# A four-branch token mixer: gate and branch products with tokens on the partitions

## The chip, the cores and the metric

The kernel runs on one core of a Trainium2 chip. The metric is the device time of one execution in microseconds. The core has TensorE (matrix products into PSUM), VectorE, ScalarE and GpSimd (elementwise work), and SyncE, which here issues all DMA.

## The reference, cut to what matters

One decoder layer, 256 tokens of 1024 channels. Four mixers A to D turn projections of x into rows of 256 channels; each is projected to 1024 channels, multiplied by a sigmoid gate, which is itself a projection of x, and the four are summed. An output projection, a residual and a layer norm follow, then 32 experts with two chosen per token, and a second layer norm.

```python
p = _split_in(x @ w_in[l])
...
ys = jnp.stack([ya, yb, yc, yd], axis=2)
gates = jax.nn.sigmoid(p["gate"].reshape(bsz, seq, N_BRANCHES, D_MODEL))
merged = jnp.sum(gates * jnp.einsum('bsnc,ncd->bsnd', ys, w_branch[l]), axis=2)
x = _layer_norm(DN_ALPHA * x + merged @ w_out[l], ln_g[l, 0], ln_b[l, 0])
y = _moe(x, ...)
x = _layer_norm(DN_ALPHA * x + y, ln_g[l, 1], ln_b[l, 1])
```

The shapes: `w_in` is 1024 x 7096, of which the last 4096 columns make the gates; `w_branch` 4 x 256 x 1024, `w_out` 1024 x 1024; the experts' three weight arrays are 32 x 1024 x 256 (two) and 32 x 256 x 1024, 96 MiB in all.

## The kernel before, in words

All data are float32. Every projection up to the router is made of three products: each operand is split in two parts (`split`, L356: ScalarE casts to the first part, L366, VectorE subtracts to the second, L367), and `mm3` (L381 to L383) issues low x high, high x low and high x high into the same PSUM bank.

The input projection's weights come as 56 tiles of 128 partitions x 1024 (`TILES`, L191), two per load. The last 32 are the gates, eight per branch in the order B, A, C, D; such a tile holds all 1024 input channels for 128 output channels. With the weights stationary and the 256 tokens of x moving, a tile takes 8 x 3 matmuls of 256 columns. Two tiles share one of the two PSUM banks of the pool `pj`; then ScalarE takes Tanh of half the value into the branch's gate tile `g` (L489), 128 channels per partition row and tokens along the row.

The branch products (`gen_M`, L1160) have the same form: stationary 128 columns of the branch's weight (split by `gen_N`, L1144), moving the branch's two-part output `parts` (256 tokens), four pieces per branch of 12 matmuls, each in a bank of the six-bank pool `px`. A piece is merged on VectorE (L1182: (gate + 1) x product) and added to the sum `mg` (L1185, GpSimd for A and C, VectorE for D). For D each piece of the sum is then split into `mgh` (L1192, ScalarE) and `mgl` (L1194, VectorE). Since channels are on the partitions, these are used as they are as stationary operands of the output projection (`gen_O`, L1313: for every one of eight channel groups 2 x 2 x 3 matmuls of 512 columns, moving the split output weights of `gen_U`).

The router (`gen_R`, one for each half of the tokens) transposes its input on TensorE (L1367), computes logits (L1384), picks experts, counts ranks (L1415) and builds selection matrices; `gen_E` gathers the rows of the first four experts (L1464). The expert loop (from L1553) takes the experts in eight groups of four. Their 1 MiB weights are loaded by `fetch` (L1247), 25 ahead: the first seven into memory that the mixers' pool gives back (step X, L1226), the next sixteen into the ring of 17 slots of 8 KB per partition (`w2`), two into smaller ones. The same 17 slots serve the weight tiles, their split parts, the gates, `parts`, `mg`, `mgh`, `mgl`, the output weights and x.

The order of all work up to the expert loop is written out: `ORDER` (L211) is a string of letters, each of which advances one generator to its next `yield` (P products of the input projection, S its splits and loads, N and M branch weights and products, D, B, A, C the mixers, L the first expert loads, U and O the output projection, Q and R the router). Every engine and SyncE's queue run their instructions in that order, each waiting for its own data and slots.

Of the kernel before, what the change touches and what calls it, by code (L numbers as in the profile page):

```python
# [113 lines left out]
def _layout(inp):  # L114
# [14 lines left out]
    for n in TILES:  # L129
# [5 lines left out]
        if n == "sm":  # L135
            c = sm
        elif n == "ck":
            c = ck
        else:
            o0 = 3000 + 1024 * "ABCD".index(n[1]) + 128 * int(n[2]) if n[0] == "g" else at[n[:-1]] + 128 * int(n[-1])  # L140
            c = W[:, o0:o0 + 128]
# [70 lines left out]
    "PSBYNDSSFSUSSXSSDPRSSQZPCDOSPEPDDDBSDDDDSPDPPDSDPDDSDPDSPPPFSDFPSPDWAFDDPPDPBSDDPDSDDBBDDDPFDDDDDPDP"  # L212
    "SDSWDPDPDBBPPWDSDSBPBBDPDSDBDPCSCDCPBPDDDWDBBMCDDBDDDBWSDSPPBWDDBBSBPDBBDPDDBWDDDDDSDDBDBDBDDBDPBDDP"
    "DBBPDDDSPDDDBDDSPDPBDDDDBDSPDDDDDBDDDDDPNNBNBDDPDDDDDDDDBPAADAANAAAADSDDDDDAASADPPAABDDABABADPBBSAAB"
    "BADADAADDDBBDBAAAAADDBDSDDBDDBBDBBPASBBBBSBBBBDPDBDPBBBCDCPBCCBBBAPSMCMCDCCCCMNCCCPCMCCMSCCCCPPSPPMN"
    "MSPNSMNPSMPSMMPMNCCSPMPSCPDDSPPPCMSSNPMCMSMMLCXPSMLLLLMPLNLNPSMMPSPLPSMMPSMMMPPSNPSPMPSPNSMMLMPPSMMM"
    "PMNPMMLNMPSMSMPMMPMSUUUUUPUMMMMMPPOUULOLLUOSULPMMLMLUUMOLOUUOUUUUOQLOQQQQQQQQQOLLQQQLQQQYYUQQRLQORRQ"
    "RLRRRRQRRRQRRZRQZQERRRRRRRRRLLLREEQQERRE"
# [3 lines left out]
def body(ctx, tc, I, out):  # L222
# [93 lines left out]
    load_tiles(2)  # L316
    SY.dma_start(cst[:, 0:CC["m2"][0]], I["cst"][:, 0:CC["m2"][0]])
    SY.dma_start(csts, I["cst"][:, NMIX:NCC])
# [110 lines left out]
    def gen_S():  # L429
# [16 lines left out]
        for i, n in enumerate(TILES):  # L446
            if i > 1:
                sh = [P, 4, 256] if n[:2] in ("av", "cv") else [P, KT, P]
# [11 lines left out]
    def gen_P():  # L460
        pair = None
        for i, n in enumerate(TILES):
# [3 lines left out]
            if n in ("av1", "cv1"):  # L466
# [8 lines left out]
                continue  # L475
            c = int(n[-1]) % 2 if n[-1].isdigit() else 0
# [5 lines left out]
            if n[0] == "g":  # L482
                m = int(n[2])
                if c:
                    yield 0
                    if m == 1:
                        gslot[n[1]] = slot("g" + n[1], [P, 4, 2, S])
                    gts[n[1], m // 2] = t = gslot[n[1]][:, m // 2]
                    A.activation(t, pair, AF.Tanh, scale=0.5)  # L489
                    if i == len(TILES) - 1:  # L490
                        ready(AF.Sqrt, t[:, 1, 0:1])
            else:
                if i == 0:
                    V.tensor_scalar(omm, pc[:, PC["mu"][0]:PC["mu"][0] + 7], -1.0, 1.0, op0=OP.mult, op1=OP.add)
                if n == "ak0":
                    G.memset(into("ak", [P, 2, 2, S]), 0.0)
# [1284 lines left out]
```

## Time and profile before

| | |
|---|---|
| Time, median of 3 runs | 511.18 us (510.54 to 512.19) |
| The profiled execution's own time | 511.06 us |
| Its span, first to last instruction | 509.3 us |
| TensorE busy | 465.8 us (91%), 4396 matmuls |
| VectorE, ScalarE, GpSimd busy | 239.1, 195.2, 46.5 us |
| DMA moved | 146.79 MB, mean 288 GB/s |
| TensorE's granted clock, mean | 0.973 of 2.4 GHz |

A record of a matmul is longer than the distance to the next one, since matmuls are pipelined: rates are read from starts, not from lengths. The DMA share is the mean busy share of the core's 16 DMA engines. SyncE's rows show when a load is issued, not when it lands. Idle time in brackets stands behind the engine that ended it.

### The profile page before, as it was taken

To read this page: it belongs to the slowest core of one execution; us is meant where nothing else is said; L and a number is where in the kernel's file an instruction comes from. 1 tells how busy PE (TensorE), PEld (TensorE's weight loads), DVE (VectorE), ACT (ScalarE), POOL (GpSimd) and SP (SyncE) were. 2 spreads that over 40 slices of the span, in tenths; PEclk is the share of its full clock that TensorE was granted. 3 is DMA by queue.
4 is the path that set the end of the run, shared out by engine and by line. 5 is a ranking of instruction groups with operands and counts; after the bars stand their busy time and mean duration, and the time that the engine had idled before them with its cause. 6 is when DMAs were issued, how large, how long until landed. Compare 5 with 4: busy or idle time off the path is not lost. (4 is left out here: it accounts for less than half of the span.)

```text
span 509.3 us, 10326 instructions
## 1 busy us (share of the span) xinstructions
PE 465.8 (91%) x4396; PEld 359.1 (71%) x4396; DVE 239.1 (47%) x479; ACT 195.2 (38%) x357; POOL 46.5 (9%) x55
## 2 busy tenths in 40 slices
PE   7999999999999999999999898998988989877891
PEld 6988888998788999999998676553635446324530
DVE  4577657976877468725665543112211122002015
ACT  5778474355586457424444242001202011101311
POOL 2101111500000011411150000000000000000002
PEclk9999999999999999999999979999999999979897
DMA  8979240340242444699679999999999999999952
GB/s 281 390 309 365 93 161 1 97 155 1 81 169 84 166 166 160 241 423 420 257 291 429 382 399 383 420 349 418 419 417 420 420 423 415 421 420 417 389 190 86
DMA packets 27416, 146.79 MB, mean 288 GB/s; under 512 B 3108, under 2 KB 5736, under 8 KB 12264
## 3 DMA queue, kind: packets, MB, share of 16 engines
q1 hardware_dynamic: 27368, 146.11, 72.8%
q8 instruction: 35, 0.57, 0.4%
q14 instruction: 13, 0.11, 0.1%
HBM read 143.48 MB, written 2.62 MB: 287 GB/s over the span
## 5 line engine op out<-in xcount | busy, mean ns | idle before, releaser
L381 PE MATMUL ps<-xl,hl 128*128 128x256 f32 x416 | 122.9, 295 | 2.3 <-ACT hl L366 1.6
L382 PE MATMUL ps<-xh,hl 128*128 128x256 f32 x416 | 119.0, 286 | 1.3 <-DVE hl L367 1.2
L383 PE MATMUL ps<-xh,hl 128*128 128x256 f32 x416 | 118.6, 285 | 0.0
L367 DVE TENSOR_TENSOR hl<-w,hl 128x1024 fp32r<-128x1024 f32 (+1 forms) x75 | 88.0, 1189 | 51.3 <-ACT hl L366 51.0
L381 PEld LDWEIGHTS ps<-xl,hl 128*128 128x128 f32 x416 | 80.7, 194 | 6.9 <-ACT hl L366 2.2
L382 PEld LDWEIGHTS ps<-xh,hl 128*128 128x128 f32 x416 | 80.7, 194 | 3.3 <-DVE hl L367 2.2
L383 PEld LDWEIGHTS ps<-xh,hl 128*128 128x128 f32 x416 | 80.7, 194 | 0.0
L366 ACT CAST hl<-w 128x1024 fp32r<-128x1024 f32 (+1 forms) x75 | 74.0, 1012 | 14.8 <-DMA w<-win 7.5
L1562 PE MATMUL ps<-w,xg 128*32 128x256 f32 x1024 | 66.6, 402 | 7.5 <-DMA w<-mwu 7.5
L1562 PEld LDWEIGHTS ps<-w,xg 128*32 128x32 f32 x1024 | 33.6, 115 | 38.1 <-DMA w<-mwu 10.1
L1464 PE MATMUL ps<-Sel,nrm 128*128 128x128 f32 x256 | 33.8, 288 | 0.9 <-DVE Sel L1457 0.9
L1464 PEld LDWEIGHTS ps<-Sel,nrm 128*128 128x128 f32 x256 | 31.4, 200 | 4.0 <-issue 3.7
L1549 PE MATMUL ps<-small,SGT 128*128 128x512 f32 x48 | 23.7, 616 | 9.3 <-DVE small L1543 5.1
L1543 DVE COPY small<-ps 128x512 f32<-128x512 f32 x6 | 4.1, 692 | 51.4 <-PE ps L1549 51.4
L1514 ACT COPY SGT<-ps 128x256 f32<-128x256 f32 x8 | 3.0, 372 | 63.3 <-PE ps L1512 63.3
L1531 PE MATMUL ps<-w,small 128*32 128x512 f32 x192 | 23.1, 598 | 3.5 <-ACT xg L1471 3.0
L1549 PEld LDWEIGHTS ps<-small,SGT 128*128 128x128 f32 x48 | 8.2, 189 | 25.0 <-DVE small L1543 10.1
L1704 POOL TENSOR_TENSOR res<-res,ln 128x512 f32<-128x512 f32 x1 | 1.6, 1646 | 235.7 <-ACT res L1703 235.7
L1457 DVE TENSOR_TENSOR Sel<-rank,csts 128x128 f32<-128x128 f32 x16 | 4.0, 289 | 31.2 <-PE ps L1512 31.1
L381 PE MATMUL ps<-parts,hl 128*128 128x256 f32 x64 | 18.6, 291 | 0.0
L382 PE MATMUL ps<-parts,hl 128*128 128x256 f32 x64 | 18.1, 283 | 0.0
L383 PE MATMUL ps<-parts,hl 128*128 128x256 f32 x64 | 18.1, 283 | 0.0
(414 smaller groups left out, 685.2 us busy)
## 6 DMA issues: line engine op xcount, KB each, us to landing
w<-mwu SPq DMA_DIRECT2D x32, 1024.0 KB, 15.0
w<-win SPq DMA_DIRECT2D x27, 1024.0 KB, 6.3
w<-mwg SPq DMA_DIRECT2D x27, 1024.0 KB, 13.6
w<-mwd SPq DMA_DIRECT2D x23, 1024.0 KB, 15.0
w<-mwd SPq DMA_DIRECT2D x10, 512.0 KB, 13.3
w<-mwg SPq DMA_DIRECT2D x10, 512.0 KB, 16.4
w<-wbr SPq DMA_DIRECT2D x4, 1024.0 KB, 5.0
w<-wout SPq DMA_DIRECT2D x4, 1024.0 KB, 6.4
```

Of the source, the lines that this page charges most:

```text
L366: A.copy(hi, src)
L367: V.tensor_tensor(lo, src, hi.bitcast(F32), op=OP.subtract)
L381: T.matmul(dst, lhsT=ls[0], rhs=rs[1], start=start, stop=False)
L382: T.matmul(dst, lhsT=ls[1], rhs=rs[0], start=False, stop=False)
L383: T.matmul(dst, lhsT=ls[0], rhs=rs[0], start=False, stop=stop)
L1457: V.tensor_tensor(t, rank[q][:, 4 * g:4 * g + 4, None].broadcast_to([P, 4, 32]), C("iota")[:, None, :].broadcast_to([P, 4, 32]), op=OP.is_ ...
L1464: T.matmul(pg[:, k4], lhsT=nrm[q][:, 128 * k:128 * k + 128], rhs=f2(SelR[g, q]), start=q == 0 and k4 == 0, stop=True, skip_group_check=True)
L1514: A.copy(SGT, pg)
L1531: T.matmul(pd[h][32 * e4:32 * e4 + 32], lhsT=outs[g][0][:, k, 32 * e4:32 * e4 + 32], rhs=wds[g][e4](k)[:, 512 * h:512 * h + 512], start=k ...
L1543: V.tensor_copy(dn[h], pd[h])
L1549: T.matmul(yacc[q, h], lhsT=outs[g][1][:, q], rhs=dn[h], start=False, stop=False, skip_group_check=True)
L1562: T.matmul(pgu[32 * e4:32 * e4 + 32, i], lhsT=xg[:, k, 32 * e4:32 * e4 + 32], rhs=ws[e4](k), start=k == 0, stop=k == KT - 1, tile_position ...
```

## The change

The packed gate weights are laid out anew: a tile now holds 256 input channels for 512 output channels, so that four tiles make one half of a branch's gates. In `gen_P` x is the stationary operand (128 channels x 128 tokens) and the weights move, 512 columns. Tile 0 and tile 1 of a four are multiplied for both halves of the tokens (6 matmuls each), tile 2 waits, and with tile 3 the two last tiles are multiplied for the first half of the tokens (12 matmuls), then for the second half. The two halves of the tokens take both banks of `pj`; Tanh is taken of each when its 12 are through.

In `gen_M` a piece is 512 channels for 128 tokens: 6 matmuls of 512 columns with `parts` as stationary operand. The sum now has tokens on the partitions, so for D each piece is transposed by four TensorE transposes into a PSUM bank, and `mgh` and `mgl` are made from that bank.

At the start one load of two weight tiles becomes two, with a load of constants between them.

`ORDER` is a new string, 644 letters instead of 640. On TensorE its stretches around the last gates are, before: gates D0 and D1, branch product C3 between them, then D0 (branch), gates D2 and D3, D1, gates D4 and D5, D2, D3, gates D6 and D7, projection step 0, and so on without a break to step 5. After: gates D0, product of C's last piece, gates D1, D's first piece, gates D2 and D3 (first and second token half), transposes of the first piece, D's second piece, gates D4, transposes of the second piece, gates D5 to D7, D's third piece, its transposes, D's fourth piece, projection step 0, transposes of the fourth piece, steps 1 to 5. On ScalarE and VectorE the split of output weight 0 stands ahead of the third piece's merge. The step X with the first expert loads stands before gate tile C0 in the old string and behind the four tiles C0 to C3 in the new one; the split of C's output stands before gate tile C0 in the old and behind C1 in the new, on VectorE behind one weight split more. Between a four's end and the next four's start stand a branch product or transposes in four of seven cases.

```diff
--- before.py
+++ after.py
@@ -136,8 +136,13 @@
             c = sm
         elif n == "ck":
             c = ck
+        elif n[0] == "g":
+
+            o0, k = 3000 + 1024 * "ABCD".index(n[1]) + 512 * (int(n[2]) // 4), 2 * (int(n[2]) % 4)
+            cols.append(W[128 * k:128 * k + 256, o0:o0 + 512].reshape(2, P, 512).transpose(1, 0, 2).reshape(P, 1024))
+            continue
         else:
-            o0 = 3000 + 1024 * "ABCD".index(n[1]) + 128 * int(n[2]) if n[0] == "g" else at[n[:-1]] + 128 * int(n[-1])
+            o0 = at[n[:-1]] + 128 * int(n[-1])
             c = W[:, o0:o0 + 128]
         cols.append(c.reshape(KT, P, P).transpose(1, 0, 2).reshape(P, 1024))
     o["win"] = np.stack(cols).reshape(len(TILES) // 2, 2, P, 1024).transpose(0, 2, 1, 3)
@@ -209,13 +214,13 @@
 SA = 1
 
 ORDER = (
-    "PSBYNDSSFSUSSXSSDPRSSQZPCDOSPEPDDDBSDDDDSPDPPDSDPDDSDPDSPPPFSDFPSPDWAFDDPPDPBSDDPDSDDBBDDDPFDDDDDPDP"
...
+    "DXSSUSDSNSSSCAQYPSRPSPDOEBZPDFPDSSSDDDDDSPDPDSPDPDPDSDDPSPBFPDPSDDFPSDPPDSDWDPSPBBBDDFDDDDSPDPDMPDDD"
...
 )
 
 
@@ -313,8 +318,10 @@
     wpart(1, 1)
     SY.dma_start(pc, I["pc"])
     SY.dma_start(lw, I["lw"])
-    load_tiles(2)
+    w_sb[2], w_sb[3] = (lambda t: (t[:, 0], t[:, 1]))(slot("w", [P, 2, 1024]))
+    SY.dma_start(w_sb[2], I["win"][1][:, 0])
     SY.dma_start(cst[:, 0:CC["m2"][0]], I["cst"][:, 0:CC["m2"][0]])
+    SY.dma_start(w_sb[3], I["win"][1][:, 1])
     SY.dma_start(csts, I["cst"][:, NMIX:NCC])
     SY.dma_start(cst[:, CC["m2"][0]:NMIX], I["cst"][:, CC["m2"][0]:NMIX])
     for i in range(4, AHEAD, 2):
@@ -445,7 +452,7 @@
         nxt = AHEAD
         for i, n in enumerate(TILES):
             if i > 1:
-                sh = [P, 4, 256] if n[:2] in ("av", "cv") else [P, KT, P]
+                sh = [P, 4, 256] if n[:2] in ("av", "cv") else [P, 2, 512] if n[0] == "g" else [P, KT, P]
                 sp[i] = split(view(w_sb.pop(i), 1024, sh), sh)
                 parts["S"] = i + 1
             while nxt < len(TILES) + KT and nxt < i + 1 + (AHEAD if i < 8 else MID if i < TI["av1"] else NEAR):
@@ -473,29 +480,43 @@
                 evacuate(n, p)
                 parts["P"] = i + 1
                 continue
+            if n[0] == "g":
+
+                m, j = int(n[2]) // 4, int(n[2]) % 4
+                if j == 0:
+                    pair = [ps([P, 512], pj) for _ in range(2)]
+
+                if j != 2:
+                    for q in range(2):
+                        for t in ((i - 1, i) if j == 3 else (i,)):
+                            h, l = sp[t]
+                            for k in range(2):
+                                kk = 2 * (t - i + j) + k
+                                mm3(pair[q], xp(kk, slice(128 * q, 128 * q + 128)), (h[:, k], l[:, k]), kk == 0, kk == KT - 1)
+                        if j == 3:
+                            yield 0
+                            if m == 0 and q == 0:
+                                gslot[n[1]] = slot("g" + n[1], [P, 2, 2, 512])
+                            gts[n[1], m, q] = t = gslot[n[1]][:, m, q]
+                            A.activation(t, pair[q], AF.Tanh, scale=0.5)
+                            if i == len(TILES) - 1 and q:
+                                ready(AF.Sqrt, t[:, 0:1])
+                    for t in ((i - 1, i) if j == 3 else (i,)):
+                        sp.pop(t)
+                parts["P"] = i + 1
+                continue
             c = int(n[-1]) % 2 if n[-1].isdigit() else 0
             if c == 0:
                 pair = ps([P, 2, S], pj)
             h, l = sp.pop(i)
             for k in range(KT):
                 mm3(pair[:, c], (h[:, k], l[:, k]), xp(k), k == 0, k == KT - 1)
-            if n[0] == "g":
-                m = int(n[2])
-                if c:
-                    yield 0
-                    if m == 1:
-                        gslot[n[1]] = slot("g" + n[1], [P, 4, 2, S])
-                    gts[n[1], m // 2] = t = gslot[n[1]][:, m // 2]
-                    A.activation(t, pair, AF.Tanh, scale=0.5)
-                    if i == len(TILES) - 1:
-                        ready(AF.Sqrt, t[:, 1, 0:1])
-            else:
-                if i == 0:
-                    V.tensor_scalar(omm, pc[:, PC["mu"][0]:PC["mu"][0] + 7], -1.0, 1.0, op0=OP.mult, op1=OP.add)
-                if n == "ak0":
-                    G.memset(into("ak", [P, 2, 2, S]), 0.0)
-                yield 0
-                evacuate(n, pair[:, c])
+            if i == 0:
+                V.tensor_scalar(omm, pc[:, PC["mu"][0]:PC["mu"][0] + 7], -1.0, 1.0, op0=OP.mult, op1=OP.add)
+            if n == "ak0":
+                G.memset(into("ak", [P, 2, 2, S]), 0.0)
+            yield 0
+            evacuate(n, pair[:, c])
             parts["P"] = i + 1
 
 
@@ -1161,39 +1182,41 @@
         parts["M"] = 0
         for b_, n in enumerate(ORDER_OF_BRANCHES):
             first, final = b_ == 0, b_ == 3
-            for jj in range(4):
-                i, j2 = jj // 2, slice(2 * (jj % 2), 2 * (jj % 2) + 2)
-                yield (n, ("N", 2 * b_ + i + 1))
-                h, l = wsp[2 * b_ + i]
-                yh, yl = parts[n]
-                pbr = ps([P, 2, S])
-                for c in range(2):
-                    cs = slice(256 * (jj % 2) + 128 * c, 256 * (jj % 2) + 128 * c + 128)
+            for i in range(2):
+                for q in range(2):
+                    yield (n, ("N", 2 * b_ + i + 1))
+                    h, l = wsp[2 * b_ + i]
+                    yh, yl = parts[n]
+                    ts_ = slice(128 * q, 128 * q + 128)
+                    pbr = ps([P, 512])
                     for k in range(2):
-                        mm3(pbr[:, c], (h[:, k, cs], l[:, k, cs]), (yh[:, k], yl[:, k]), k == 0, k == 1)
-                parts["M"] += 1
-                yield TI[f"g{n}{2 * jj + 1}"] + 1
-                g = gts.pop((n, jj))
-                if first and jj % 2 == 0:
-                    if i == 0:
-                        t = slot("mg", [P, 2, 4, S])
-                        mg.extend((t[:, 0], t[:, 1]))
-                dst = mg[i][:, j2]
-                V.scalar_tensor_tensor(f2(dst) if first else f2(g), in0=f2(g), scalar=1.0, in1=f2(pbr), op0=OP.add, op1=OP.mult)
-                if not first:
-                    yield 0
-                    (V if final else G).tensor_tensor(dst, dst, g, op=OP.add)
-                if final:
-                    yield 0
-                    if jj == 0:
-                        for m in range(2):
-                            t = slot("mg" + "hl"[m], [P, 2, 4, S], dt=F32R)
-                            mgs[m].extend((t[:, 0], t[:, 1]))
-                    A.copy(mgs[0][i][:, j2], dst)
-                    yield 0
-                    V.tensor_tensor(mgs[1][i][:, j2], dst, mgs[0][i][:, j2].bitcast(F32), op=OP.subtract)
-                    if jj % 2:
-                        parts["mg%d" % i] = True
+                        mm3(pbr, (yh[:, k, ts_], yl[:, k, ts_]), (h[:, k], l[:, k]), k == 0, k == 1)
+                    parts["M"] += 1
+                    yield TI[f"g{n}{4 * i + 3}"] + 1
+                    g = gts.pop((n, i, q))
+                    if first and i == 0 and q == 0:
+
+                        mg.append(slot("mg", [P, 2, 2, 512]))
+                    dst = mg[0][:, i, q]
+                    V.scalar_tensor_tensor(dst if first else g, in0=g, scalar=1.0, in1=pbr, op0=OP.add, op1=OP.mult)
+                    if not first:
+                        yield 0
+                        (V if final else G).tensor_tensor(dst, dst, g, op=OP.add)
+                    if final:
+                        yield 0
+                        if i == 0 and q == 0:
+                            for m in range(2):
+                                t = slot("mg" + "hl"[m], [P, 2, 4, S], dt=F32R)
+                                mgs[m].extend((t[:, 0], t[:, 1]))
+                        pt = ps([P, 4, P])
+                        for k in range(4):
+                            T.transpose(pt[:, k], dst[:, 128 * k:128 * k + 128], ident)
+                        yield 0
+                        A.copy(mgs[0][i][:, :, ts_], pt)
+                        yield 0
+                        V.tensor_tensor(mgs[1][i][:, :, ts_], pt, mgs[0][i][:, :, ts_].bitcast(F32), op=OP.subtract)
+                        if q:
+                            parts["mg%d" % i] = True
 
     def gen_W():
 
```

## Rows read from the trace of the kernel before

**Rows 1.** The page, part 2: forty slices, busy tenths.

```profile
PE   7999999999999999999999898998988989877891
DMA  8979240340242444699679999999999999999952
```

**Rows 2.** The chain of waits: start us, us, what.

```profile
343.50 16.88 DMA w<-mwu
...
451.60 19.93 DMA w<-mwu
```

**Rows 3.** Windows: us, then PE, PEld, DVE, ACT, POOL busy, PEclk, DMA share, GB/s.

```profile
215.00:220.00 5.00, 5.00 (x44) 5.00 (x43) 0.90 (x1) 1.42 (x2) 2.05 (x1) 1.00 1.01 419
...
245.00:250.00 5.00, 5.00 (x44) 5.00 (x43) 2.61 (x3) 3.05 (x5) 0.00 (x0) 1.00 0.38 157
...
260.00:265.00 5.00, 5.00 (x41) 4.87 (x40) 4.08 (x5) 1.84 (x4) 4.60 (x7) 1.00 0.49 203
...
295.00:300.00 5.00, 4.82 (x24) 4.68 (x23) 2.24 (x12) 1.95 (x2) 0.00 (x0) 0.50 0.99 382
...
345.00:455.00 110.00, 94.88 (x972) 48.25 (x974) 17.85 (x56) 15.32 (x38) 0.00 (x0) 0.98 1.01 420
```

**Rows 4.** Timeline of SyncE's queue, loads issued: start us, us, what.

```profile
207.80 2.26 SPq L1264 DMA_DIRECT2D w<-mwg  x4
...
255.72 1.15 SPq L248 DMA_DIRECT2D w<-wout  x2
264.12 1.28 SPq L1264 DMA_DIRECT2D w<-mwd  x3
...
289.95 7.38 SPq L1264 DMA_DIRECT2D w<-mwd  x5
```

**Rows 5.** Timeline of TensorE, gate products, the first and the thirtieth in sequence.

```profile
214.78 0.28 PE L381 MATMUL ps<-xl,hl 128*128 128x256 f32 x1
...
218.26 0.28 PE L383 MATMUL ps<-xh,hl 128*128 128x256 f32 x1
```

**Rows 6.** Timeline of TensorE, output projection: two rows 21 steps apart, and the last.

```profile
267.36 0.39 PE L383 MATMUL ps<-hl,mgh 128*128 128x512 f32 x1
...
272.12 0.39 PE L383 MATMUL ps<-hl,mgh 128*128 128x512 f32 x1
...
289.30 0.40 PE L383 MATMUL ps<-hl,mgh 128*128 128x512 f32 x1
```

**Rows 7.** Timeline of TensorE in the router: transposes, gathers, first expert product.

```profile
283.58 0.66 PE L1367 MATMUL ps<-csts,xtok 128*128 128x128 f32 x4 [0.16 <-DVE xtok L1360]
...
296.31 3.79 PE L1464 MATMUL ps<-Sel,nrm 128*128 128x128 f32 x16 [0.18 <-DVE Sel L1457]
...
301.06 2.02 PE L1464 MATMUL ps<-Sel,nrm 128*128 128x128 f32 x16 [0.70 <-DVE Sel L1457]
303.01 1.29 PE L1562 MATMUL ps<-w,xg 128*32 128x256 f32 x20
```

**Rows 8.** Timeline of VectorE, the merge of D's third piece.

```profile
262.81 0.67 DVE L1182 SCALAR_TENSOR_TENSOR gD<-gD,ps 128x512 f32<-128x512 f32 x1
263.52 0.69 DVE L1185 TENSOR_TENSOR mg<-mg,gD 128x512 f32<-128x512 f32 x1
264.89 0.69 DVE L1194 TENSOR_TENSOR mgl<-mg,mgh 128x512 fp32r<-128x512 f32 x1 [0.69 <-ACT mgh L1192]
```

**Rows 9.** Timeline of ScalarE: one Tanh and one cast of a split.

```profile
259.55 0.59 ACT L489 ACTIVATE gD<-ps 128x512 f32<-128x512 f32 x1
260.04 1.04 ACT L366 CAST hl<-w 128x1024 fp32r<-128x1024 f32 x1
```

**Rows 10.** Timeline of VectorE: the split of C's output.

```profile
205.92 1.79 DVE L532 TENSOR_TENSOR parts<-yC,parts 128x512 fp32r<-128x512 f32 x1
```

**Rows 11.** Windows of 20 us, the first and the last of fourteen.

```profile
0.00:20.00 20.00, 16.77 (x79) 14.76 (x80) 9.22 (x18) 11.43 (x21) 3.75 (x13) 0.91 0.89 317
...
260.00:280.00 20.00, 20.00 (x107) 17.23 (x106) 13.79 (x15) 10.39 (x14) 4.60 (x7) 1.00 0.87 355
```

More of the change, by code (lines that the diff above doesn't have):

```diff
@@ L211 @@
 ORDER = (
-    "PSBYNDSSFSUSSXSSDPRSSQZPCDOSPEPDDDBSDDDDSPDPPDSDPDDSDPDSPPPFSDFPSPDWAFDDPPDPBSDDPDSDDBBDDDPFDDDDDPDP"
[L213 to L218, printed above, removed]
+    "DXSSUSDSNSSSCAQYPSRPSPDOEBZPDFPDSSSDDDDDSPDPDSPDPDPDSDDPSPBFPDPSDDFPSDPPDSDWDPSPBBBDDFDDDDSPDPDMPDDD"
+    "PSDDDDDSDPWBPPBWDDPSBPBSBWDDPFBDDBCCSCCPBDPDWBDBDDSDDBDDDSPDBPBWDBBSDDPDDBPBDBDDDWDBBDDSDPBDDBDPBBDD"
+    "DPDDDBDSDPDDDPBSDPDDDBDDPDSDDDDBDDDDBDDDDPDPNNDSDBDDPABDDDAAAAADDANAAABDNDDBDPDDBBASBABDBBDPAADADASA"
+    "AADDPBDAADABDAADBDBDBSDBDAPDDBBBBSBABSBBBBBPDPBDBPCBCDBCCBBBACCACCBPSCCMMCCCCCASMNCPMMDSCCCSPNCDPCCD"
+    "PSMPSPCSCDPSLDPPCMNPSPMMNPMMPSSMNPMMNPMSPMSPPSCMPPMPXLLLLMSSMPMNNPMLMSLSMMLMPNPMPSSNPPMPMMMPSSMSNMPP"
+    "LSPLPMMMMMMMMSPNMSUUUMPMPPPUUPSMMMMMLLLMMOLMMUMUUOUUMMOUUOOUULLOUUULLUOQOOQQQQQQQQRQLQQOQLQLRQQQRRYQ"
+    "QQRRYRRQURRRRQRQRZRQZLRRRRELRRRRLREQEEQRRELL"
 )
```

## The prediction, made before the change was timed

> **What bounds the kernel now.** I read the page's forty slices first. TensorE is at 9 tenths in nearly every slice, but the DMA row is at 0 to 4 from 50 to 190 us and at 9 from 216 us on: two regimes, and a handover between them [rows 1]. The chain of waits, read back from the end, is expert-weight DMA from 343.50 to 471.53 us, each transfer released by the one before, and small TensorE work before that [rows 2]. So the stretches are needed next. From 345 to 455 us the DMA share is 1.01 at 420 GB/s. From 215 to 245 it is also full (row 215:220 stands for six), but from 245 to 265 the first of four windows of 5 us has 0.38 and the last 0.49: summed over the four, 7.0 us of idle DMA, while TensorE is busy for every microsecond [rows 3]. SyncE's list shows why: after two output weights at 255.72 the next load, expert weights, goes out only at 264.12, when the last gate product has left its slots; after that the loads follow one another closely. At 289.95, just after the output projection's last matmul at 289.30, the loads again wait for slots [rows 4, 6]. From this I read: until about 290 us TensorE's products set the time (they free the slots), after it the rate at which the weights arrive. A microsecond taken from TensorE before 290 us should come out at the end almost whole; DMA that is early before that gains nothing, since its slots fill.
>
> **Gate and branch products.** Before, 32 gate tiles x 8 x 3 = 768 matmuls of 256 columns and 16 x 2 x 2 x 3 = 192 for the branches. Their starts stand 29 apart from 214.78 to 218.26 us: 120.0 ns each, at granted clock 1.00 [rows 3, 5]. After: 384 and 96 matmuls of 512 columns. That shape, with the same three-part product, runs in the output projection: 21 steps from 267.36 to 272.12 us, 226.7 ns each [rows 6]. So 512 columns cost 226.7 instead of 240 ns, a fixed part of 13.3 ns per matmul. Gates: 384 x 13.3 ns = 5.1 us, branches 96 x 13.3 ns = 1.3 us, together -6.4 us. Nothing hides this, as TensorE is busy throughout these stretches [rows 3]. Below, this part saves nothing (rival d); above, it can't exceed the 13.3 ns by the rows, and I take -6.4.
> The Trainium skill's "TensorE: Matmul & The Clock Gate", section "Back-to-back issue gap", has a warm isolated gap of N/2.4 + 2.5 ns; as an estimate from it, halving 960 matmuls would save 480 x 2.5 ns = 1.2 us and the sum below would be +2.9 us. The trace's 13.3 ns disagrees, and the measurement decides.
>
> **Transposes.** 16 are added on TensorE. The router's four take 0.66 us with 0.28 us for the last one's own record, so starts are (0.66 - 0.28) / 3 = 127 ns apart [rows 7]: +2.0 us, all in a full stream. Below: 16 x 120 ns = 1.9 us; above, each alone at 282 ns, 4.5 us.
> The same page's section "Part 4: PE-mode transpose" gives about 275 ns for one in a kernel's context; 16 of them would be an estimated 4.4 us and the sum +0.1 us. Rows 7 agree with this as the length of one record but not as the distance between starts, and I go by the latter.
>
> **The last merges.** Before, the merges of D (multiply 0.67, add 0.69, copy, subtract 0.69 us) lie beside gate products and the projection's first half, and TensorE waits for none of them [rows 8]. In the new order D's third and fourth branch products stand behind the last gate products, and after the third one TensorE's next instruction is the transpose of its merged rows; the fourth product and the whole projection are queued behind it. It waits for the product's last end (0.16 us behind its slot, 0.39 - 0.227 [rows 6]), 0.67 + 0.69 us of VectorE and some 0.1 us of signals: 1.6 us. If the split of the first output weight (cast 1.04 [rows 9], subtraction about 1.2 us), which stands ahead of the multiply on ScalarE and VectorE, can only start when the last gate product frees its slot, it is 1.04 + 1.2 + 0.1 + 0.67 + 0.69 + 0.2 - 1.36 = 2.5 us (1.36 us being the third product itself, six steps). I take 2.1, the middle. The three other groups of transposes have a product of 2.7 us between merge and transpose and cost no wait; with that cover gone each would cost 1.6 us. The later copy and subtract of D's fourth piece stand behind two casts, but the projection's steps 0 to 3 (4 x 12 x 0.227 = 10.9 us) lie in between.
>
> **PSUM.** Before, two tiles fill one of two banks, so a bank's Tanh has 48 matmuls = 5.8 us. After, four tiles fill both; the next group's second half needs the second Tanh 6 x 0.227 = 1.36 us after the group's end. Tanh 0.60 us plus 0.28 us for the matmul's end fits if ScalarE is free, so I cost it at nothing; a cast (1.04 us) in front of it at each of the 7 boundaries makes 7 x (0.60 + 0.28 + 1.04 - 1.36) = 3.9 us [rows 5, 9]. In the new order four of these boundaries also have a branch product (1.36 us) between.
>
> **Memory and loads.** The expert stream starts at 207.80 us, as VectorE's split of C's output (205.92, 1.79 us) is through [rows 4, 10]. In the new order the stream's step stands four gate tiles later, but these loads wait for data, not for TensorE's place: that split follows the end of A's gates by the same distance plus one more subtraction of 1.2 us. Gates of B and A and six branch products end 2.6 + 0.5 us earlier, so the stream starts about 2 us earlier; if it waited for those four tiles, 11.5 - 3 = 8.5 us later, of which 7.0 us could be taken out of the idle DMA of 245 to 265 us. The third tile of a group is held for one tile more, and at the group's end two splits' slots come free at once; the number of slots and loads is the same. At the start SyncE issues half of one weight load (the tile that is used fourth) behind a constant: nothing, as three tiles of 2.9 us come before it. The other steps are reordered from the first microsecond: in fourteen windows of 20 us up to 280 us TensorE idles 5.6 us, 3.2 of them in the first [rows 11], so there is at most 2.4 us to gain and I allow as much to lose; I take 0.
>
> **Sum.** -6.4 + 2.0 + 2.1 = -2.3 us against the profiled execution's 511.06 us (span 509.3 plus 1.8 around it), which lies 0.1 us under the median of 511.18: predicted 508.9 us. A difference under 0.3% (1.5 us) can't be told from none here.
>
> **Rivals.**
> (a) More is gained at the end. The last gate product ends some 8 us earlier (6 us saved, two branch products of 1.4 us each moved behind it, transposes against), so the loads of 264.12 us go out near 256 us, into DMA that idles. For it: the 7.0 us of idle DMA. Against it: the slots after it are freed by the projection, whose end moves by 2 us only. If half of the idle time is regained beyond my shift: 508.9 - 3 = 506 us.
> (b) The gain is used up: the wait before the transposes at its upper end (+0.4) and one more such wait (+1.6), -0.3 in sum; or each transpose costs its whole record (4.5 instead of 2.0 us), +0.2; or the granted clock, which was 0.50 from 295 to 300 us and made sixteen gather matmuls take 3.79 instead of 2.02 us [rows 3, 7], falls over one more such group, -0.5. Each ends at about 511 us. For it: the waits are in the order of steps. Against it: the rows give each a smaller middle.
> The Trainium skill's 275 ns per transpose (above) is the second of these, an estimated 511.2 us.
> (c) Slower, by the PSUM banks: ScalarE works in order, and a cast that waits for its slot or its load stands ahead of the second Tanh. Place: the 7 boundaries between groups. Price: two casts ahead give 7 x (0.88 + 2.08 - 1.36) = 11.2 us at most, one gives 3.9. It turns the sign when a boundary waits more than 2.3 / 7 = 0.33 us. At one cast: 508.9 + 3.9 = 512.8 us. Against it: ScalarE is busy for 1.4 to 3.1 of 5 us in the rows before 250 us [rows 3].
> (d) The fixed part stays: the gate stream's step depends on columns alone, so 512 columns cost 240 ns and nothing is saved. Then +2.0 + 2.1 = +4.1: 515.3 us. Against it: rows 6, the same shape.
> By the Trainium skill's 2.5 ns (above) 1.2 us of this would still be saved, an estimated 514.1 us; the rows speak against it as against (d).
>
> **How the numbers follow.** The forecast has 0.46; (a) 0.18; (b) 0.18; (c) 0.14; (d) 0.04. Of the forecast 0.34 lies below -1.5 us and 0.12 within; (a) is faster; of (b) 0.04 faster, 0.14 same; of (c) 0.02 same and 0.12 slower; (d) slower. So faster 0.56, same 0.28, slower 0.16. The likeliest case alone spans 507 to 510.5 us (waits 1.6 to 2.5, reordering +-1.5). The range goes from 505.0, (a) with all of the 7 us short of the slots' limit, to 513.0, (c) at one cast per boundary: it leaves out what lies beyond (a), two casts, and (d).
>
> **What would show it.** Right: gate and branch matmuls of 512 columns starting 227 ns apart; 16 transposes of 127 ns steps; one TensorE gap of 1.6 to 2.5 us before the ninth to twelfth of them; the projection's last matmul and the first expert product (before at 303.01 us) 2 to 3 us earlier; DMA full from there on, with the same distance to the end. Wrong: idle TensorE of half a microsecond at group ends with ScalarE's Tanh as releaser (c), steps of 240 ns (d), idle DMA after 290 us, or an end that moves by another amount than the first expert product.

## The result, and the profile after

The changed kernel takes 503.02 us (median of four runs, 501.77 to 504.63) against 511.19 us of the kernel before: ratio 0.984 [0.9806, 0.9875], 8.2 us faster. Two later measures of the same kernel, six runs each, gave 504.26 us (ratio 0.987 [0.9844, 0.9897]) and 504.80 us (0.9878 [0.985, 0.9906]): 6.4 and 6.6 us faster, and I take some 6.5 us as the gain. The forecast was 508.9 us with a range from 505.0: all three medians lie under the range. The profiled execution of the changed kernel took 504.63 us, its span is 502.8.

The forty slices, busy tenths, of the changed kernel:

```profile
PE   7999999999999999999989899998988989875891
DMA  7998342112342444799899889999999999999942
```

TensorE is as full as before, and the DMA row is full a little earlier [rows 1]. The windows (us; PE, PEld, DVE, ACT, POOL busy; granted clock, DMA share, GB/s) show that the hole before 265 us has shrunk: the DMA share from 245 to 250 us was 0.38 and is 0.87, from 260 to 265 us it was 0.49 and is 1.02. Idle DMA comes back behind it: in this execution the share is 0.74 from 275 to 280 us, 0.82 from 285 to 290 us and 0.61 from 300 to 305 us. From 345 us on it is full, as before [rows 3]:

```profile
215.00:220.00 5.00, 5.00 (x23) 4.13 (x22) 2.82 (x2) 0.96 (x2) 2.42 (x2) 1.00 1.00 419
245.00:250.00 5.00, 5.00 (x24) 4.14 (x23) 1.50 (x2) 0.62 (x2) 0.00 (x0) 1.00 0.87 300
260.00:265.00 5.00, 5.00 (x25) 4.13 (x24) 4.97 (x5) 3.31 (x4) 0.00 (x0) 1.00 1.02 419
345.00:455.00 110.00, 95.80 (x1016) 51.74 (x1020) 20.25 (x63) 15.49 (x39) 0.00 (x0) 1.00 1.01 419
```

SyncE's queue: the stream of expert weights starts 4.9 us earlier, the loads behind the last gate product 12.1 us earlier [rows 4]. Of both, 1.8 us come from the start (table below); counted from the norm's first product they are 3.1 and 10.4 us earlier, in the second and third profile as well:

```profile
202.91 2.28 SPq L1287 DMA_DIRECT2D w<-mwg  x4
...
251.99 1.28 SPq L1287 DMA_DIRECT2D w<-mwd  x3
...
281.83 9.03 SPq L1287 DMA_DIRECT2D w<-mwd  x5
```

TensorE's gate products, twelve in sequence: 2.49 us for eleven steps, 226.4 ns each, the projection's rate [rows 5, 6]:

```profile
215.71 0.39 PE L388 MATMUL ps<-hl,xh 128*128 128x512 f32 x1
...
218.20 0.39 PE L390 MATMUL ps<-hl,xh 128*128 128x512 f32 x1
```

TensorE around D's third piece: the last product of the piece, the transpositions behind a wait of 1.51 us (1.67 us lost against the product's own step), the first projection product, the last one, and the first expert product [rows 6, 7]:

```profile
253.15 0.39 PE L390 MATMUL ps<-hl,parts 128*128 128x512 f32 x1
255.05 0.66 PE L1213 MATMUL ps<-csts,mg 128*128 128x128 f32 x4 [1.51 <-DVE mg L1204]
255.46 0.47 PE L388 MATMUL ps<-hl,parts 128*128 128x512 f32 x1
...
256.93 0.40 PE L388 MATMUL ps<-hl,mgh 128*128 128x512 f32 x1
...
281.21 0.40 PE L390 MATMUL ps<-hl,mgh 128*128 128x512 f32 x1
...
297.31 1.97 PE L1585 MATMUL ps<-w,xg 128*32 128x256 f32 x24
```

VectorE in that wait: the split of the output weight ends at 253.18, and the merge starts when the product is through, at 253.58 [rows 8]:

```profile
251.95 1.23 DVE L374 TENSOR_TENSOR hl<-w,hl 128x1024 fp32r<-128x1024 f32 x1 [5.45 <-ACT hl L373]
253.58 0.69 DVE L1201 SCALAR_TENSOR_TENSOR gD<-gD,ps 128x512 f32<-128x512 f32 x1 [0.41 <-PE ps L390]
254.30 0.69 DVE L1204 TENSOR_TENSOR mg<-mg,gD 128x512 f32<-128x512 f32 x1
```

To find where the time went I cut every span at three events on TensorE: the first product of the first mixer's norm (24.78 us before, 23.02 after), the last projection product, and the first expert product. Times in us; the ratio is against runs of the kernel before on the same chip.

| kernel | median | ratio | start to norm | norm to projection's last | to first expert | to the end |
|---|---|---|---|---|---|---|
| before | 511.19 | | 24.78 | 264.52 | 13.71 | 206.3 |
| changed | 503.02 | 0.984 | 23.02 | 258.19 | 16.10 | 205.5 |
| e10 changed again | 504.26 | 0.987 | 25.08 | 258.21 | 13.97 | 205.0 |
| e14 changed, third | 504.80 | 0.9878 | 24.67 | 258.19 | 13.89 | 206.0 |
| e1 order alone | 509.35 | 0.9977 | 26.15 | 262.09 | 13.90 | 205.7 |
| e13 order again | 508.37 | 0.9952 | 25.05 | 262.11 | 14.11 | 205.2 |
| e11 half the order | 511.56 | 1.0019 | 24.41 | 264.19 | 13.73 | 206.2 |
| e15 halves | 509.68 | 0.9962 | 25.08 | 264.07 | 14.94 | 205.6 |
| e7 thrice | 508.91 | 0.9956 | 24.45 | 261.70 | 13.96 | 207.8 |
| e2 undivided load | 503.41 | 0.9878 | 24.21 | 258.22 | 13.85 | 205.2 |
| e3 old first letters | 505.48 | 0.992 | 24.89 | 258.39 | 14.03 | 203.2 |
| e4 step 0 as cover | 505.32 | 0.9919 | 25.34 | 260.61 | 14.94 | 205.5 |
| e5 early product | 504.45 | 0.9859 | 26.66 | 257.68 | 15.10 | 205.6 |
| e6 nine warm-ups | 503.89 | 0.9858 | 22.81 | 258.46 | 13.83 | 205.3 |
| e8 both | 503.00 | 0.9838 | 23.80 | 257.39 | 14.04 | 205.2 |
| e12 both again | 503.22 | 0.985 | 25.10 | 257.74 | 15.35 | 205.0 |
| e9 before, nine | 509.68 | 0.9995 | 23.24 | 264.44 | 15.09 | 205.2 |

The stretch from the norm to the projection's last product repeats to 0.1 us where a kernel was profiled more than once (0.35 us in e8 and e12, which are one kernel). It falls from 264.5 to 258.2 us, but 0.8 us of that is work that only moved: the new order has eight of the router's logit products behind the projection's last product, the old one (and e11) has them in front of it. Between kernels of different order the fair measure is the sum up to the first expert product: 278.23 us before, 272.18 and 272.08 us in e10 and e14, whose router had a like clock (0.84, 0.83 and 0.83 from 280 to 300 us): 6.1 us, nearly the whole gain. The start and the router's stretch vary by more than 2 us with the granted clock, whichever kernel it is, and what follows the first expert product is 205.0 to 206.3 us in all but two.

### The profile page after: what moved, and what is told of

Same layout as the page of the kernel before. It is cut to its first block, busy times and chain, and to the rows that moved or that the text cites. A ratio compares the mean times of both kernels' runs of the same rounds, so it can differ in the third digit from the quotient of the medians.

```text
span 502.8 us, 9400 instructions
## 1 busy us (share of the span) xinstructions
PE 459.7 (91%) x3932; PEld 334.1 (66%) x3932; DVE 242.7 (48%) x479; ACT 195.0 (39%) x357; POOL 47.5 (9%) x55
## 5 line engine op out<-in xcount | busy, mean ns | idle before, releaser
L374 DVE TENSOR_TENSOR hl<-w,hl 128x1024 fp32r<-128x1024 f32 (+1 forms) x75 | 93.7, 1262 | 34.7 <-ACT hl L373 34.2
L388 PE MATMUL ps<-hl,xh 128*128 128x512 f32 (+1 forms) x160 | 60.8, 380 | 0.0
L390 PE MATMUL ps<-hl,xh 128*128 128x512 f32 (+1 forms) x160 | 58.9, 368 | 0.0
L389 PE MATMUL ps<-hl,xl 128*128 128x512 f32 (+1 forms) x160 | 58.9, 368 | 0.0
L388 PE MATMUL ps<-xl,hl 128*128 128x256 f32 x160 | 47.4, 296 | 2.7 <-DVE xl L374 2.1
L389 PE MATMUL ps<-xh,hl 128*128 128x256 f32 x160 | 45.6, 285 | 0.2 <-DVE hl L374 0.2
L390 PE MATMUL ps<-xh,hl 128*128 128x256 f32 x160 | 45.2, 282 | 0.0
L1487 PE MATMUL ps<-Sel,nrm 128*128 128x128 f32 x256 | 35.5, 297 | 0.9 <-DVE smr L1451 0.7
L388 PEld LDWEIGHTS ps<-xl,hl 128*128 128x128 f32 x160 | 30.6, 191 | 6.6 <-ACT hl L373 2.5
L388 PEld LDWEIGHTS ps<-hl,xh 128*128 128x128 f32 x160 | 30.2, 188 | 5.8 <-issue 0.7
L389 PEld LDWEIGHTS ps<-hl,xl 128*128 128x128 f32 x160 | 30.2, 189 | 5.2 <-issue 0.5
L390 PEld LDWEIGHTS ps<-hl,xh 128*128 128x128 f32 x160 | 30.2, 189 | 5.1
L389 PEld LDWEIGHTS ps<-xh,hl 128*128 128x128 f32 x160 | 30.6, 191 | 1.1 <-DVE hl L374 0.9
L390 PEld LDWEIGHTS ps<-xh,hl 128*128 128x128 f32 x160 | 30.6, 191 | 0.0
```

Source lines behind the costliest of these rows:

```text
L374: V.tensor_tensor(lo, src, hi.bitcast(F32), op=OP.subtract)
L388: T.matmul(dst, lhsT=ls[0], rhs=rs[1], start=start, stop=False)
L389: T.matmul(dst, lhsT=ls[1], rhs=rs[0], start=False, stop=False)
L390: T.matmul(dst, lhsT=ls[0], rhs=rs[0], start=False, stop=stop)
L1487: T.matmul(pg[:, k4], lhsT=nrm[q][:, 128 * k:128 * k + 128], rhs=f2(SelR[g, q]), start=q == 0 and k4 == 0, stop=True, skip_group_check=True)
```

## The experiments

**Order alone (e1, e13).** The products of the kernel before with the new order, less the four letters of the transpositions.

```diff
 ORDER = (
-    "PSBYNDSSFSUSSXSSDPRSSQZPCDOSPEPDDDBSDDDDSPDPPDSDPDDSDPDSPPPFSDFPSPDWAFDDPPDPBSDDPDSDDBBDDDPFDDDDDPDP"
+    "DXSSUSDSNSSSCAQYPSRPSPDOEBZPDFPDSSSDDDDDSPDPDSPDPDPDSDDPSPBFPDPSDDFPSDPPDSDWDPSPBBBDDFDDDDSPDPDMPDDD"
...
```

> The products of before (weights stationary, 256 tokens moving, no transposes) under the new order of steps, less its four letters for the transposes; loads at the start as before. Theory O (the missing 6 us come from the new order: waits between the mixers' steps and at the start are gone, so the order alone is worth 3 to 4.5 us): 506.7 to 508.2 us. Theory S (the products are worth more than my rows said and the order nothing): 510 to 512 us. Theory C (the granted clock, 1.2 GHz for 3.4 us at the start of the profiled run of before and for none in that of after, makes the difference): the time follows the mean clock of each run, 509.5 us where the start is at 2.4 GHz, 511 where it is not.

Ratio 0.9977 [0.9955, 1.0], so 0 to 2.3 us faster; the two medians on that chip, 509.35 and 509.21 us, show nothing, and Theory O's 3 to 4.5 us are not reached. The trace tells more: TensorE reaches the first expert product 2.2 us sooner after the norm (275.99 for 278.23 us). Three waits of the kernel before are gone from its timeline, and for the fourth, in the router, there is one of 0.60 us at the next transpositions, since the eight logit products now fill its place. The four in the kernel before:

```profile
137.16 0.34 PE L818 MATMUL ps<-VUz,tm_be 128*64 128x64 f32 x4 [0.39 <-DVE VUz L809]
...
142.52 1.12 PE L847 MATMUL ps<-yD,cst 128*128 128x512 f32 x2 [0.46 <-ACT yD L843]
...
233.94 0.39 PE L382 MATMUL ps<-xh,hl 128*128 128x256 f32 x1 [0.87 <-DVE hl L367]
...
290.87 0.63 PE L1367 MATMUL ps<-csts,xtok 128*128 128x128 f32 x4 [1.17 <-DVE xtok L1360]
```

By distance of starts (from the product before the wait to the one behind it, less the usual step) they cost 0.56, 0.62, 1.04 and (1.34 - 0.77) 0.57 us, 2.8 us together. A new one stands before the projection's second step, where the order has put the split of its output weight behind D's merges; below it is the one that is left in the router (both order alone):

```profile
267.06 0.50 PE L381 MATMUL ps<-hl,mgh 128*128 128x512 f32 x1 [1.30 <-DVE hl L367]
...
291.85 0.63 PE L1367 MATMUL ps<-csts,xtok 128*128 128x128 f32 x4 [0.60 <-DVE xtok L1360]
```

The new one costs 1.46 us. A fifth wait of the kernel before is gone too: the 0.16 us in front of the router's first transpositions at 283.58 us [rows 7], 0.32 us by starts. The remaining 0.5 us are spread over the mixers' small products, without idle time in front of them; I found no one place for them, and their cause stays open. The repeat, beside the changed kernel:

> The new order with the products of the kernel before (without the four letters of the transpositions), a second time, now beside the changed kernel on one chip. Theory 1 (the order's own gain, which the trace gives as 2.2 us up to the first expert product, reaches the end): 2 to 2.5 us under the kernel before, 3.8 above the changed one. Rival 2 (the order gains nothing in time, and the products alone make the difference): within 1 us of the kernel before and some 5.5 us above the changed one.

Ratio 0.9952 [0.9931, 0.9973]: 1.4 to 3.5 us faster, and 3.6 us above the changed kernel of the same chip. That is Theory 1's split, and the stretch to the projection's last product is the same as in e1 (262.11 us).

**Changed again (e10, e14).** No edit.

> The changed kernel once more, beside the others on one chip, so that they can be compared directly. Theory 1 (its four runs so far were lucky at the start): 504 to 505 us, 6 to 6.5 us under the kernel before. Rival 2 (the first measure holds): 503 us, 8 us under.

> The changed kernel, a third time, as the base of this comparison: 6 to 6.5 us under the kernel before, as in the second measure.

504.26 and 504.80 us, 6.4 and 6.6 us under the kernel before: Theory 1's number. That the first four runs were lucky is shown in part only. Their mean granted clock was 0.976, against 0.975 and 0.974 here, which by the 3 us per 0.01 at the end of this text makes 0.3 to 0.6 us; the rest of the difference stays open.

**Products cut back to 256 columns (e15).**

```diff
-                                mm3(pair[q], xp(kk, slice(128 * q, 128 * q + 128)), (h[:, k], l[:, k]), kk == 0, kk == KT - 1)
+                                for e in (slice(0, 256), slice(256, 512)):
+                                    mm3(pair[q][:, e], xp(kk, slice(128 * q, 128 * q + 128)), (h[:, k, e], l[:, k, e]), kk == 0 and not e.start, kk == KT - 1 and e.start > 0)
...
-                        mm3(pbr, (yh[:, k, ts_], yl[:, k, ts_]), (h[:, k], l[:, k]), k == 0, k == 1)
+                        for e in (slice(0, 256), slice(256, 512)):
+                            mm3(pbr[:, e], (yh[:, k, ts_], yl[:, k, ts_]), (h[:, k, e], l[:, k, e]), k == 0 and not e.start, k == 1 and e.start > 0)
```

> The changed kernel with each of its 480 gate and branch products of 512 columns cut in two of 256; weights, transpositions, merges and order are the same. It puts back 480 fixed parts and nothing else. Theory 1 (12.2 ns each by the mean steps of the trace, 239.6 - 227.4; TensorE one to one): 5.9 us above the changed kernel, so about the kernel before: the order's gain then only makes up for transpositions and waits. Theory 2 (the prediction's 13.3 ns): 6.4 us above. Rival 3 (part of the products' gain is lost before the end): under 4.5 us above; the trace's last projection product moves by more than the time.

The stretch grows from 258.19 to 264.07 us, by 5.88: Theory 1's number. The time grows by 4.9 us (509.68 against 504.80; by the ratios 4.3 us, some 1.7 uncertain), which does not tell Theory 1 from Rival 3 by itself. The stretch is the cleanest measure of the products' part, as order and transpositions stay, and the wait before the ninth transposition too (1.57 us idle for 1.51).

**Transpositions three times (e7).**

```diff
-                        for k in range(4):
+                        for k in (0, 1, 2, 3) * 3:
```

> The changed kernel with each of D's 16 transpositions made three times into the same place: 32 more. Theory 1 (1.47 us for the 16 by distance of starts, so 0.09 us each, and TensorE sets the time one to one): 2.9 us above the changed kernel, about 506. By the prediction's 127 ns: 4.1 us above. By the length of one record, 0.28 us each: 9 us above. Rival 2 (the loads set the end): the output projection ends some 3 us later and the end stays within 0.5 us of 503.0.

```profile
240.25 1.49 PE L1213 MATMUL ps<-csts,mg 128*128 128x128 f32 x12
...
258.24 1.53 PE L1213 MATMUL ps<-csts,mg 128*128 128x128 f32 x12 [1.51 <-DVE mg L1204]
```

Twelve in a row: (1.49 - 0.28) / 11 = 110 ns a step. The stretch grows by 3.5 us, 0.11 each, and the ratio by 0.0086 against e10's (4.4 us, some 1.8 uncertain): TensorE's time comes out at the end, and Rival 2 falls. The Trainium skill's "TensorE: Matmul & The Clock Gate", section "Part 4: PE-mode transpose", has about 275 ns for one; by it 32 more would be an estimated 8.8 us, and neither the stretch nor the time shows that.

**Undivided load (e2) and old first letters (e3).** In e2 one line loads both tiles again; e3 has the old order's first 280 letters (up to the first gate product), then what is left of the new one.

```diff
-    w_sb[2], w_sb[3] = (lambda t: (t[:, 0], t[:, 1]))(slot("w", [P, 2, 1024]))
-    SY.dma_start(w_sb[2], I["win"][1][:, 0])
+    load_tiles(2)
     SY.dma_start(cst[:, 0:CC["m2"][0]], I["cst"][:, 0:CC["m2"][0]])
-    SY.dma_start(w_sb[3], I["win"][1][:, 1])
```

> The changed kernel with the third and fourth weight tile in one load again, ahead of the constants. In the two profiles the first 16 us differ by 1.8 us. If the divided load makes that: 504.8 us. If it is the granted clock at the start, or the order: 503.0 us, within 0.5.

> The changed kernel with the first 280 letters of the old order (all up to the first gate product), then the rest of the new order. Theory O: the 2 us that the first 110 us are shorter belong to the order, so 505 us. Theory S or C: 503 us, within 0.7; with C the start's clock decides run by run.

e2: ratio 0.9878, the changed kernel's own; the divided load is worth nothing that can be told. e3: 0.992 [0.9889, 0.9951], whose interval touches the changed kernel's; its stretch is 258.39 us, so if the old first letters cost anything, it isn't there. That stays open.

**First half of the new order (e11).** Old products; 371 letters of the new order, then what is left of the old.

```diff
 ORDER = (
-    "PSBYNDSSFSUSSXSSDPRSSQZPCDOSPEPDDDBSDDDDSPDPPDSDPDDSDPDSPPPFSDFPSPDWAFDDPPDPBSDDPDSDDBBDDDPFDDDDDPDP"
+    "DXSSUSDSNSSSCAQYPSRPSPDOEBZPDFPDSSSDDDDDSPDPDSPDPDPDSDDPSPBFPDPSDDFPSDPPDSDWDPSPBBBDDFDDDDSPDPDMPDDD"
...
```

> The kernel before with its own products, and of the new order only the first 371 letters, up to B's first branch product; then what is left of the old order. From the norm's first product to the projection's last one the kernel before takes 264.5 us and the one with the whole new order 262.1. Theory 1 (the order gains where TensorE waits end: 0.39 and 0.46 us in D's scan, in this half; 0.87 us for the slot of an output weight's split, in the other): 263.3 us, the wait near 233 us still there and the 1.3 us wait in the projection not, and the end some 1 us below the kernel before. Rival 2 (the gain lies in the order around the last gates): 264.5 us and the time of before. Rival 3 (the whole gain of the order is in this half, and the other half only trades a wait for another): 262 us or less.

264.19 us and no gain in time (ratio 1.0019 [1.0001, 1.0037]): Rival 2's number, but not for its reason. The two waits in D's scan (137.16 and 142.52 us) are gone, two others have come in C's (0.37 and 0.62 us by starts), and the one near 233 us is left:

```profile
165.71 0.73 PE L1117 MATMUL ps<-qat,Sc 128*64 128x64 f32 x8 [0.21 <-DVE Sc L1103]
166.90 0.28 PE L1117 MATMUL ps<-qat,Sc 128*64 128x64 f32 x2 [0.46 <-DVE Sc L1105]
```

```profile
233.27 0.39 PE L382 MATMUL ps<-xh,hl 128*128 128x256 f32 x1 [0.75 <-DVE hl L367]
```

So the first half can't be priced by itself: with the rest of the old order behind it, it brings waits that the whole new order doesn't have.

**The wait before the transpositions (e4, e5).** e4 moves the projection's step 0 ahead of them (one letter O); e5 puts D's third branch product between the token halves of the last gates.

```diff
-    "LSPLPMMMMMMMMSPNMSUUUMPMPPPUUPSMMMMMLLLMMOLMMUMUUOUUMMOUUOOUULLOUUULLUOQOOQQQQQQQQRQLQQOQLQLRQQQRRYQ"
+    "LSPLPMMMMMMMMSPNMSUUUMPMPPPUUPSMMMOMMLLLMMLMMUMUUOUUMMOUUOOUULLOUUULLUOQOOQQQQQQQQRQLQQOQLQLRQQQRRYQ"
...
-    "LSPLPMMMMMMMMSPNMSUUUMPMPPPUUPSMMMMMLLLMMOLMMUMUUOUUMMOUUOOUULLOUUULLUOQOOQQQQQQQQRQLQQOQLQLRQQQRRYQ"
+    "LSPLPMMMMMMMMSPNMSUUUMPMPMPPMMUUPSMMLLLMMOLMMUMUUOUUMMOUUOOUULLOUUULLUOQOOQQQQQQQQRQLQQOQLQLRQQQRRYQ"
```

> The changed kernel with the output projection's step 0 (12 matmuls, 2.7 us) put ahead of the transposes of D's third piece, so that TensorE has work while VectorE merges. The wait there was 1.51 us in the profile. If TensorE sets the time up to the router, as I predicted: 501.5 us. If slots or the DMA set it there: 503.0 us. The fourth piece's transposes then have no product in front of them, and would wait themselves: 503.0 us as well, with the gap 5 us later in the trace.

> The changed kernel, with D's third branch product put between the two token halves of the last four gate tiles (its merge directly behind the Tanh of the first half), so that the 12 gate products of the second half (12 x 0.227 = 2.7 us) lie beside the merge. Theory 1 (TensorE sets the time up to the router one to one): the gap of 1.67 us ahead of the ninth transposition goes and no other takes its place; the output projection and the end come some 1.5 us earlier than in the changed kernel, about 501.5 us. Rival 2 (the loads set the end, a microsecond taken there is not seen): the gap goes from the trace, the end stays at 503 us. Rival 3 (as in the run with the projection's first step as cover): the wait moves on to the fourth piece and the end is at 503 us or above.

In e4 the third piece no longer waits, the fourth does:

```profile
258.54 0.60 PE L1213 MATMUL ps<-csts,mg 128*128 128x128 f32 x4
262.13 0.63 PE L1213 MATMUL ps<-csts,mg 128*128 128x128 f32 x4 [1.60 <-DVE mg L1204]
```

By starts that is 1.77 us, a wait of 0.66 us for an output weight follows behind these transpositions, and the old wait's 1.67 us are saved: 0.8 us more. The stretch is 2.4 us longer than the changed kernel's. The other 1.7 us come from the granted clock, which in this execution was 0.51 from 264.2 to 267.6 us, right behind the two waits (1.00 there in the changed kernel). The wait moved as the last of the expectations has it; the time, 505.32 us, is above each of them and 1.9 us above e2's on the same chip, with intervals that overlap. In e5 there are two smaller ones, 0.42 us before the fourth piece's transpositions and 0.66 behind them for an output weight; the first is this row:

```profile
262.11 0.63 PE L1213 MATMUL ps<-csts,mg 128*128 128x128 f32 x4 [0.26 <-DVE mg L1204]
```

The stretch is 0.5 us shorter (257.68) than the changed kernel's, not 1.5: Rival 3 in part. The ratio, 0.9859, is the changed kernel's within its interval.

**More warm-up (e6, e8, e9, e12).** e6 and e9 are the changed kernel and the one before with one constant changed; e8 and e12 are e5 with the same.

```diff
-WARM = 5
+WARM = 9
```

> The changed kernel with nine instead of five warm-up products ahead of the first weight products, in time in which TensorE has no data yet. Theory 1 (a part of the gain of 8.2 us is the granted clock at the start, which the kernel before had at 0.5 to 0.6 from 10 to 14 us and the changed one at 1.00): where the changed kernel also has such a stretch in some of its runs, more work ahead takes it away, and the median is 0.5 to 1 us lower. Rival 2: the profile of the start stays as in the changed kernel and the time is the same, 503.0 us. Rival 3: the added products delay the first weight products, at most 4 x 0.23 = 0.9 us later.

> Both at once: D's third branch product between the token halves, and nine warm-up products. Theory 1: the gains add, 500.5 to 501.5 us, faster than both kernels. Rival: 503 us, as neither counts.

> The kernel before with nine instead of five warm-up products and nothing else changed. Theory 1 (the stretch at half clock from 10 to 14 us costs some 1.7 us in most runs of either kernel, and four products more at the start take it away): the same gain as the changed kernel with nine has over the changed kernel, 1 to 2 us, about 508 to 509; the profile shows clock 1.00 from 2 to 20 us. Rival 2 (the changed order makes the start safe, the warm-up does nothing): as before, 510 us or more.

> The changed kernel with D's third branch product between the token halves and nine warm-up products, once more beside the changed kernel on one chip. Theory 1 (1.1 us of TensorE's time up to the projection's end, and the stretch at half clock at the start): 2 us below the changed kernel, about 502 to 503. Rival: no difference that five rounds can tell.

Theory 1 of e9 isn't borne out, and e6 can't tell: its ratio is 0.9858 [0.9827, 0.9888], the changed kernel's within its interval. The clock at the start was 1.00 in the profiles of e6, e8 and e9, but e9's ratio is 0.9995 [0.9973, 1.0016], and in e12, the same kernel as e8, the start lost its clock all the same. e8 took 503.00 us, its rival's number; the gains that Theory 1 adds up did not come. e12 beside e10: ratios 0.985 [0.9827, 0.9874] and 0.987 [0.9844, 0.9897]; its stretch is 0.5 us shorter. It is faster than the kernel before, but whether it beats the changed one these runs can't tell.

## Why the prediction was wrong, step by step

| term of the sum | predicted | measured |
|---|---|---|
| products of 512 columns | -6.4 | -5.9 (e15) |
| 16 transpositions | +2.0 | +1.5 (by starts); 0.11 each in e7 |
| wait at the last merges | +2.1 | +1.7 (the gap at 253.15) |
| PSUM banks | 0 | 0 |
| start of the stream, divided load | 0 | 0 |
| new order of steps | 0 | -3.6 (e1, e13: -2.1, and 1.46 for a wait of their own) |
| sum | -2.3 | -6.3; measured between norm and first expert product, router at a like clock: 278.2 to 272.1, -6.1 |

**The step that failed is "reorder 0".** I had seen that TensorE idles 2.4 us between 20 and 280 us [rows 11] and allowed that much each way, but took zero. The order with the old products (e1, e13) gains 2.1 us up to the first expert product though it carries a wait of 1.46 us of its own, which the changed kernel doesn't have: -2.1 - 1.5 = -3.6. Of these, 2.8 are the four waits shown above and 0.3 the fifth. Three of them lie within the 2.4 us I had counted (0.39 + 0.46 + 0.87 = 1.72 of idle time; 2.22 by distance of starts, since a record outlasts its slot by 0.16 us and the idle column doesn't count that). The fourth, 1.17 us, and the fifth stood in the router, past the 280 us at which my table of windows ended. The last 0.5 us show no idle time at all. So the bound of 2.4 us was wrong as well as the zero: idle time up to 280 us does not limit what an order can gain. I could have asked each wait by name whether the new order keeps it; I gave all of them one sentence and a zero.

**The products** were read rightly: 512 columns start 226.4 ns apart in the rows above and 227.4 as the mean of the 372 gate products (of 384) that have the next one straight behind them, 256 columns 119.9 before; e15's 5.88 us are 12.2 ns for each of 480, instead of 13.3. Rival (d) falls. The Trainium skill's "TensorE: Matmul & The Clock Gate", section "Back-to-back issue gap", has a fixed part of 2.5 ns in its isolated gap; by it e15 would be an estimated 480 x 2.5 ns = 1.2 us longer, and it is 5.88.

**The wait** came where it was put, before the ninth to twelfth transpositions, and at its lower end: the split of the output weight was through 0.4 us before the product, so my 2.5 us case did not arise. Counted against the order alone it is nearly free, 1.67 instead of 1.46 us. The later pieces did not wait. **Transpositions** cost 0.36 us for four, less than 4 x 127 ns; my rate from three steps of the router [rows 7] was too high.

**PSUM banks**, rival (c): the timeline has no idle TensorE at a group's end. **The regimes** were right: the first expert product comes 5.7, 5.8 and 6.3 us earlier in the three profiles of the changed kernel (2 to 3 us were forecast), these executions are 6.4, 7.0 and 6.5 us shorter than the profiled one before, and the last column of the table is the same within 1.3 us. The prediction's sign against itself, idle DMA after 290 us, shows all the same: a share of 0.61 from 300 to 305 us in the first of the three, of 0.84 and 0.94 from 290 to 295 us in e10 and e14 (1.01 before). **Rival (a)** named 506 us, but its mechanism is not what happened: the stream started 3.1 us earlier from the norm on (not 2), the loads of 264.12 us did go out at 251.99, into DMA that had idled, and yet up to the first expert product the DMA had moved 69.6, 69.0 and 69.1 MB (234, 232 and 233 GB/s), against 69.4 MB (229 GB/s) before. What went out earlier waited later, and the end still stands 205 to 206 us behind the first expert product.

**The range** ended at 505.0 because I let (a) alone set its lower end; a gain from the order had no place there.

## What to carry to other kernels

When a change brings a new order of steps, list the bound engine's waits in the profile one by one, router and all, and ask of each whether the new order still has what it waits for; a zero for the whole order needs a reason, and idle time alone doesn't bound it. Price a wait by the distance of starts. A wait that the change adds may stand in place of one that the order has anyway, and what is moved to cover it can hand it to the next piece, as e4 and e5 show.

## What the runs showed of the hardware that was not expected

TensorE's granted clock falls to half (1.2 GHz) for a few us near the start of 13 of the 17 profiled executions, of either kernel, after a stretch in which TensorE waits for its first data. The changed kernel, first profile and second, from 10 to 14 us:

```profile
10.00:14.00 4.00, 4.00 (x33) 3.81 (x33) 2.93 (x9) 2.46 (x5) 0.00 (x0) 1.00 1.03 416
```

```profile
10.00:14.00 4.00, 3.66 (x18) 3.46 (x19) 2.93 (x7) 2.20 (x4) 0.00 (x0) 0.63 1.02 412
```

From 2 to 10 us TensorE had been busy for 5.76 and 5.37 us. Such a stretch moves the norm's first product by some 2 us (23.02 and 25.08). It doesn't depend on the warm-up alone: with nine warm-ups and 6.67 us busy e12 fell to 0.67, e9 with 7.41 us stayed at 1.00. Nor does it follow the busy time alone: the kernel before had 6.23 us and fell to 0.57. The router's clock varies too: in the first profile of the changed kernel it was 0.66 from 280 to 300 us, where the stretch to the first expert product took 16.10 instead of 13.9 us, in the second 0.83. Over all runs on record a kernel's time on one chip follows its mean granted clock, about 3 us for 0.01 by a straight line, which explains 58% of the variance. A stretch of the trace that has the same clock in both kernels tells a change of 1 us where the medians can't.
